# Depthwise 3x3 convolution on one core: the taps' column edges cut out of the matmuls instead of being subtracted afterwards

## The chip, the cores and the metric

The kernel runs on one core of a Trainium2 chip. The metric is device time in microseconds (us), the median of several runs. The kernel before takes 208.08 us (four runs, 207.67 to 208.5).

## What is computed

For each of 16 images and each of 128 channels (`groups = channels`, so no sum over channels) a 64x64 picture is convolved with its own 3x3 filter, zero padded by one:

```python
x_pad = np.pad(x, ((0, 0), (0, 0), (1, 1), (1, 1)))
for kh in range(3):
    for kw in range(3):
        output[b, c] += weight[c, 0, kh, kw] * x_pad[b, c, kh:kh+64, kw:kw+64]
```

A term (kh, kw) of this sum is called a tap below, written (dh, dw) as in the code. Input and output are float32.

## The kernel before

The 128 channels lie on the 128 partitions, and one image at a time is worked on. An image is loaded as one DMA that casts float32 to float16, into a row of 4096 elements (64 rows of 64) with 2 zeros in front and 2 behind (`xf`, L38 and L67 to L71; three buffers). The nine taps are shared out among three engines:

- Six taps (`PE_TAPS`, L31: all that shift by a column) are matmuls with a diagonal 128x128 matrix (`dmega`, made at the start by VectorE from an identity matrix that GpSimd writes). The image is done in two halves of 32 rows. A half is one PSUM tile `ps` of four banks (two such tiles in all, L45, which is the whole PSUM); each tap is four matmuls of 8 rows, 24 per half, 48 per image (L107). The matmul reads 512 elements in one run, shifted by one element for a column shift. At a row's end this shift reads the neighbouring row's element where the reference has a zero.
- Two taps (`ACT_TAPS`, L32: centre column, upper and lower row) are scaled copies on ScalarE into `t16` (L83; four buffers).
- The centre tap is on VectorE: `acc = xf * w + ps`, one instruction per half, which also empties PSUM (L116 for half 0, L124 for half 1).

VectorE then subtracts what the matmuls took from the neighbouring row: for each of the six taps one instruction over a single column of 63 or 64 elements, stride 64, with the negated weight `wneg` (L144). Then it adds the two ScalarE tiles (L154, twice), and GpSimd issues the store of the whole image, cast to float32 (L161; `acc` has three buffers).

Loads and stores are all issued by GpSimd, in program order of that engine: two small memsets of the pad, the load, and later the store. The order within each engine is written down at build time by a planner, which may move an instruction past others of the same engine. In the profile VectorE does image b in the order L116, second L154 of image b-1, L124, six L144, first L154. Semaphores between engines are placed by the same framework, which derives them from which instruction reads and writes which tile.

Of the kernel before, what the change touches and what calls it, by code (L numbers as in the profile page):

```python
# [1 line left out]

# [5 lines left out]


F32 = mybir.dt.float32
F16 = mybir.dt.float16


@with_exitstack
def kernel(
    ctx: ExitStack,
    tc: tile.TileContext,
    x: bass.AP,
    weight: bass.AP,  # L20
    out: bass.AP,
):
    nc = tc.nc

    B, C, H, W = x.shape
    KH = weight.shape[2]
    KW = weight.shape[3]
    assert C == 128 and KH == 3 and KW == 3 and H == 64 and W == 64
    HW = H * W

    PE_TAPS = [(1, 0), (1, 2), (0, 0), (0, 2), (2, 0), (2, 2)]  # L31
    ACT_TAPS = [(0, 1), (2, 1)]  # L32

    RG = 8
    NRG = 4
    HALF = RG * NRG

    XPAD = 2  # L38
    XLEN = XPAD + HW + 2

    consts = ctx.enter_context(tc.tile_pool(name="consts", bufs=1))
    xpool = ctx.enter_context(tc.tile_pool(name="xp", bufs=3))
    apool = ctx.enter_context(tc.tile_pool(name="acc", bufs=3))
    tpool = ctx.enter_context(tc.tile_pool(name="tt", bufs=4))
    pspool = ctx.enter_context(tc.tile_pool(name="ps", bufs=2, space=bass.MemoryType.PSUM))  # L45

    ident = consts.tile([128, 128], F32, name="ident")
    make_identity(nc, ident)

    wt = consts.tile([128, 16], F32, name="wt")  # L50
    nc.sync.dma_start(
        out=wt[:, 0:9], in_=weight.rearrange("c o kh kw -> c (o kh kw)")
    )
    wt16 = consts.tile([128, 16], F16, name="wt16")
    nc.vector.tensor_copy(out=wt16[:, 0:9], in_=wt[:, 0:9])  # L55
    wneg = consts.tile([128, 16], F32, name="wneg")
    nc.vector.tensor_scalar_mul(wneg[:, 0:9], wt16[:, 0:9], -1.0)  # L57

    dmega = consts.tile([128, 9, 128], F16, name="dmega")
    for (dh, dw) in PE_TAPS:  # L60
        k = dh * 3 + dw
        nc.vector.tensor_scalar_mul(dmega[:, k, :], ident, wt[:, k : k + 1])  # L62

    def tap_rows(dh):
        return max(0, 1 - dh), H - max(0, dh - 1)

    for b in range(B):  # L67
        xf = xpool.tile([128, XLEN], F16, name="xf")
        nc.gpsimd.memset(xf[:, 0:XPAD], 0.0)  # L69
        nc.gpsimd.memset(xf[:, XPAD + HW : XLEN], 0.0)  # L70
        nc.gpsimd.dma_start(  # L71
            out=xf[:, XPAD : XPAD + HW], in_=x[b].rearrange("c h w -> c (h w)")
        )

        acc = apool.tile([128, H, W], F16, name="acc")

        act_t = []
        for (dh, dw) in ACT_TAPS:
            k = dh * 3 + dw
            deh = dh - 1  # L80
            lo, hi = tap_rows(dh)
            t16 = tpool.tile([128, H, W], F16, name="t16")
            nc.scalar.activation(  # L83
                out=t16[:, lo:hi, :],
                in_=xf[:, XPAD + (lo + deh) * W : XPAD + (hi + deh) * W],
                func=mybir.ActivationFunctionType.Copy,
                scale=wt[:, k : k + 1],
            )
            act_t.append((t16, lo, hi))

        ps_tiles = []
        for half in range(2):
            hbase = half * HALF
            ps = pspool.tile([128, HALF, W], F32, name="ps")
            ps_tiles.append(ps)
            ntaps = len(PE_TAPS)
            for ti, (dh, dw) in enumerate(PE_TAPS):
                k = dh * 3 + dw
                deh = dh - 1
                dew = dw - 1  # L100
                lo, hi = tap_rows(dh)
                for rg in range(NRG):
                    r0 = max(hbase + rg * RG, lo)
                    r1 = min(hbase + rg * RG + RG, hi)
                    src = XPAD + (r0 + deh) * W + dew
                    n = (r1 - r0) * W
                    nc.tensor.matmul(  # L107
                        ps[:, r0 - hbase : r1 - hbase, :],
                        dmega[:, k, :],
                        xf[:, src : src + n],  # L110
                        start=(ti == 0),
                        stop=(ti == ntaps - 1),
                    )

        kC = 4
        nc.vector.scalar_tensor_tensor(  # L116
            out=acc[:, 0:HALF, :],
            in0=xf[:, XPAD : XPAD + HALF * W],
            scalar=wt[:, kC : kC + 1],
            in1=ps_tiles[0][:, :, :],  # L120
            op0=mybir.AluOpType.mult,
            op1=mybir.AluOpType.add,
        )
        nc.vector.scalar_tensor_tensor(  # L124
            out=acc[:, HALF:H, :],
            in0=xf[:, XPAD + HALF * W : XPAD + HW],
            scalar=wt[:, kC : kC + 1],
            in1=ps_tiles[1][:, :, :],
            op0=mybir.AluOpType.mult,
            op1=mybir.AluOpType.add,  # L130
        )

        for (dh, dw) in PE_TAPS:
            k = dh * 3 + dw
            deh = dh - 1
            lo, hi = tap_rows(dh)
            if dw == 0:
                col = 0
                src0 = XPAD + (lo + deh) * W - 1
            else:  # L140
                col = W - 1
                src0 = XPAD + (lo + deh) * W + W
            n = hi - lo
            nc.vector.scalar_tensor_tensor(  # L144
                out=acc[:, lo:hi, col : col + 1],
                in0=xf[:, src0 : src0 + (n - 1) * W + 1 : W],
                scalar=wneg[:, k : k + 1],
                in1=acc[:, lo:hi, col : col + 1],
                op0=mybir.AluOpType.mult,
                op1=mybir.AluOpType.add,  # L150
            )

        for (t16, lo, hi) in act_t:
            nc.vector.tensor_tensor(  # L154
                out=acc[:, lo:hi, :],
                in0=acc[:, lo:hi, :],
                in1=t16[:, lo:hi, :],
                op=mybir.AluOpType.add,
            )

        nc.gpsimd.dma_start(out=out[b], in_=acc)  # L161


# [1 line left out]
_INS = ['x', 'weight']  # L165
_OUTS = [((16, 128, 64, 64), 'float32')]


# [23 lines left out]
```

## Time and profile before

| what | us |
|---|---|
| median of four runs | 208.08 |
| the profiled execution's own time | 207.67 |
| its span, from first to last instruction | 205.7 |
| first load issued / landed | 1.34 / 9.36 |
| first matmul | 9.50 |
| last matmul ends (174.62 + 10.55) | 185.17 |
| last store issued | 197.10 |

The span holds three stretches: 9.5 us until the first image is there, some 176 us in which matmuls run, and 20.5 us behind the last matmul. In the long middle stretch an image takes 11.08 to 11.09 us, seen as the distance between one memset of the pad and the next on GpSimd. The 1.97 us between span and time lie outside of what the trace shows.

### The profile page before, as it was taken

To read this page: it belongs to the slowest core of one execution; us is meant where nothing else is said; L and a number is where in the kernel's file an instruction comes from. 1 tells how busy PE (TensorE), PEld (TensorE's weight loads), DVE (VectorE), ACT (ScalarE), POOL (GpSimd) and SP (SyncE) were. 2 spreads that over 40 slices of the span, in tenths; PEclk is the share of its full clock that TensorE was granted. 3 is DMA by queue.
4 is the path that set the end of the run, shared out by engine and by line. 5 is a ranking of instruction groups with operands and counts; after the bars stand their busy time and mean duration, and the time that the engine had idled before them with its cause. 6 is when DMAs were issued, how large, how long until landed. Compare 5 with 4: busy or idle time off the path is not lost.

```text
span 205.7 us, 1985 instructions
## 1 busy us (share of the span) xinstructions
PE 169.7 (82%) x768; PEld 74.1 (36%) x768; DVE 175.8 (85%) x168; ACT 117.9 (57%) x33; POOL 19.8 (10%) x70
## 2 busy tenths in 40 slices
PE   0199999999998989898999989898989898990000
PEld 0044444444443434343434434343434343440000
DVE  2004899999999999999999999999999999999920
ACT  2199658484848576775848484848677674800000
POOL 5000011111111101011111111110101110101010
PEclk9999999999999999999999999999999999999555
DMA  4995069999999999999999999899999993452745
GB/s 71 215 215 112 0 99 300 285 237 352 209 384 182 408 182 379 198 351 233 293 284 279 315 239 343 177 424 175 386 198 347 233 333 156 175 233 102 306 204 204
DMA packets 4761, 50.46 MB, mean 245 GB/s; under 512 B 656, under 2 KB 656, under 8 KB 656
## 3 DMA queue, kind: packets, MB, share of 16 engines
q0 software_dynamic: 4608, 50.33, 84.3%
q8 instruction: 6, 0.10, 0.2%
q1 hardware_dynamic: 144, 0.00, 0.0%
q14 instruction: 3, 0.02, 0.0%
HBM read 33.56 MB, written 33.55 MB: 326 GB/s over the span
## 4 chain that ended last, share of the span: by engine, by line
DVE 43%; issue 42%; PE 6%; DMA 4%; POOL 1%; POOLq 0%; DVEq 0%
DVE acc L154 15%; DVE acc L124 14%; DVE acc L144 12%; PE ps L107 6%; DMA xf<-in_x_dram 4%; DVE acc L116 1%; POOL out_dram L161 1%; POOLq L187 0%; DVEq L154 0%; DVEq L144 0%; POOL ident masks.py:197 0%; POOL xf L69 0%; POOL xf L70 0%; POOLq L161 0%; POOLq masks.py:199 0%
## 5 line engine op out<-in xcount | busy, mean ns | idle before, releaser
L107 PE MATMUL ps<-xf,dmega 128*128 128x512 f16 (+1 forms) x768 | 169.7, 380 | 15.5 <-DMA xf<-in_x_dram 9.5
L83 ACT ACTIVATE t<-xf,wt 128x4032 f16<-128x4032 f16 x32 | 116.7, 3654 | 60.1 <-DVE acc L154 54.4
L107 PEld LDWEIGHTS <-dmega 128*128 128x128 f16 x768 | 74.1, 98 | 110.6 <-DVE acc L116 11.6
L154 DVE TENSOR_TENSOR acc<-acc,t 128x4032 f16<-128x4032 f16 x32 | 72.2, 2256 | 1.8
L116 DVE SCALAR_TENSOR_TENSOR acc<-xf,wt,ps 128x2048 f16<-128x2048 f16 x16 | 37.5, 2342 | 12.4 <-PE ps L107 12.4
L124 DVE SCALAR_TENSOR_TENSOR acc<-xf,wt,ps 128x2048 f16<-128x2048 f16 x16 | 37.5, 2343 | 2.8 <-PE ps L107 2.8
L144 DVE SCALAR_TENSOR_TENSOR acc<-xf,wneg,acc 128x63 f16<-128x63 f16 (+1 forms) x96 | 30.9, 532 | 1.6
L161 POOL DMA_DIRECT2D out_dram<-acc x16 | 8.6, 536 | 105.2 <-DVE acc L154 105.2
L71 POOL DMA_DIRECT2D xf<-in_x_dram x16 | 8.7, 542 | 4.9 <-issue 4.9
L69 POOL MEMSET xf<- 128x2 f16 x16 | 1.7, 105 | 67.2 <-DVE acc L144 63.5
L83 ACT ACT_TABLE_LOAD x1 | 1.3, 1283 | 2.4 <-DMA wt<-in_weight_dram 2.4
L55 DVE CAST wt<-wt 128x9 f16<-128x9 f32 x1 | 0.2, 185 | 2.3 <-DMA wt<-in_weight_dram 2.3
L70 POOL MEMSET xf<- 128x2 f16 x16 | 1.6, 99 | 0.0
L62 DVE TENSOR_SCALAR dmega<-ident,wt 128x128 f16<-128x128 f32 x6 | 1.3, 297 | 0.0
masks.py:199 POOL TENSOR_SCALAR_AFFINE_SELECT ident<-ident 128x128 f32<-128x128 f32 x1 | 0.3, 304 | 0.1
masks.py:197 POOL MEMSET ident<- 128x128 f32 x1 | 0.2, 204 | 0.3 <-POOLq L176 0.3
L57 DVE TENSOR_SCALAR wneg<-wt 128x9 f32<-128x9 f16 x1 | 0.2, 174 | 0.0
L176 POOL MEMSET const-float32-0.0<- 128x1 f32 x1 | 0.1, 98 | 0.2 <-issue 0.2
L176 POOL MEMSET const-float32-1.0<- 128x1 f32 x1 | 0.1, 98 | 0.0
L176 POOL MEMSET const-bfloat16-1.0<- 128x1 bf16 x1 | 0.1, 98 | 0.0
L176 POOL MEMSET const-uint8-127<- 128x1 uint8 x1 | 0.1, 98 | 0.0
## 6 DMA issues: line engine op xcount, KB each, us to landing
out_dram<-acc POOLq DMA_DIRECT2D x16, 2048.0 KB, 6.6
xf<-in_x_dram POOLq DMA_DIRECT2D x16, 1024.0 KB, 8.0
wt<-in_weight_dram SPq DMA_DIRECT2D x1, 4.5 KB, 1.6
```

Of the source, the lines that this page charges most:

```text
L62: nc.vector.tensor_scalar_mul(dmega[:, k, :], ident, wt[:, k : k + 1])
L69: nc.gpsimd.memset(xf[:, 0:XPAD], 0.0)
L70: nc.gpsimd.memset(xf[:, XPAD + HW : XLEN], 0.0)
L71: nc.gpsimd.dma_start(out=xf[:, XPAD : XPAD + HW], in_=x[b].rearrange("c h w -> c (h w)"))
L83: nc.scalar.activation(out=t16[:, lo:hi, :], in_=xf[:, XPAD + (lo + deh) * W : XPAD + (hi + deh) * W], func=mybir.ActivationFunctionType.Copy,
L107: nc.tensor.matmul(ps[:, r0 - hbase : r1 - hbase, :], dmega[:, k, :], xf[:, src : src + n], start=(ti == 0), stop=(ti == ntaps - 1),)
L116: nc.vector.scalar_tensor_tensor(out=acc[:, 0:HALF, :], in0=xf[:, XPAD : XPAD + HALF * W], scalar=wt[:, kC : kC + 1], in1=ps_tiles[0][:, : ...
L124: nc.vector.scalar_tensor_tensor(out=acc[:, HALF:H, :], in0=xf[:, XPAD + HALF * W : XPAD + HW], scalar=wt[:, kC : kC + 1], in1=ps_tiles[1] ...
L144: nc.vector.scalar_tensor_tensor(out=acc[:, lo:hi, col : col + 1], in0=xf[:, src0 : src0 + (n - 1) * W + 1 : W], scalar=wneg[:, k : k + 1] ...
L154: nc.vector.tensor_tensor(out=acc[:, lo:hi, :], in0=acc[:, lo:hi, :], in1=t16[:, lo:hi, :], op=mybir.AluOpType.add,)
L161: nc.gpsimd.dma_start(out=out[b], in_=acc)
L176: nc = _bacc.Bacc("TRN2", target_bir_lowering=False, num_devices=1)
```

## The change

Three things are changed.

First, the column shift. A matmul of a tap with dw = 0 now writes only columns 1 to 63 of its 8 rows, one with dw = 2 only columns 0 to 62, so input and output are 8 runs of 63 elements and nothing has to be subtracted: the six instructions of L144 go. For the rows' edges the pad in front of and behind the image becomes 66 elements of zeros, so that every matmul has all of its 8 rows. The tap (0, 1), which needs no cut, goes to TensorE, as its first tap; (0, 0) goes to ScalarE, which writes columns 1 to 63 into one of three tiles of their own whose column 0 is set to zero once at the start (`tedge`). The adds and copies go over 4096 elements where they went over 4032.

Second, the first image's load is cut in two DMAs: 34 rows, then 30.

Third, the last image is finished and stored by halves: per half the centre tap, two adds over half of the tile, and a store of half the image.

```diff
-    PE_TAPS = [(1, 0), (1, 2), (0, 0), (0, 2), (2, 0), (2, 2)]
-    ACT_TAPS = [(0, 1), (2, 1)]
+    PE_TAPS = [(0, 1), (1, 0), (1, 2), (0, 2), (2, 0), (2, 2)]
+    ACT_TAPS = [(0, 0), (2, 1)]
...
-    XPAD = 2
-    XLEN = XPAD + HW + 2
+    XPAD = W + 2
+    XLEN = XPAD + HW + W + 2
...
+    tedge = []
+    for i in range(3):
+        te = consts.tile([128, H, W], F16, name=f"tedge{i}")
+        nc.vector.memset(te[:, :, 0:1], 0.0)
+        tedge.append(te)
...
+        xsrc = x[b].rearrange("c h w -> c (h w)")
+        if first:
+            nsplit = (HALF + 2) * W
+            nc.gpsimd.dma_start(out=xf[:, XPAD : XPAD + nsplit], in_=xsrc[:, 0:nsplit])
+            nc.gpsimd.dma_start(out=xf[:, XPAD + nsplit : XPAD + HW], in_=xsrc[:, nsplit:HW])
+        else:
+            nc.gpsimd.dma_start(out=xf[:, XPAD : XPAD + HW], in_=xsrc)
...
-            lo, hi = tap_rows(dh)
-            t16 = tpool.tile([128, H, W], F16, name="t16")
+            lo = 1 if dw == 0 else 0
+            t16 = tedge[b % 3] if dw == 0 else tpool.tile([128, H, W], F16, name="t16")
+            xrow = xf[:, XPAD + deh * W : XPAD + deh * W + HW]
             nc.scalar.activation(
-                out=t16[:, lo:hi, :],
-                in_=xf[:, XPAD + (lo + deh) * W : XPAD + (hi + deh) * W],
+                out=t16[:, :, lo:W],
+                in_=xrow.rearrange("c (h w) -> c h w", w=W)[:, :, 0 : W - lo],
...
+                lo, hi_c = (1, W) if dw == 0 else (0, W - 1) if dw == 2 else (0, W)
                 for rg in range(NRG):
...
+                    base = XPAD + (hbase + rg * RG + dh - 1) * W
+                    rows = xf[:, base : base + RG * W].rearrange("c (r w) -> c r w", w=W)
                     nc.tensor.matmul(
-                        ps[:, r0 - hbase : r1 - hbase, :],
+                        ps[:, rg * RG : rg * RG + RG, lo:hi_c],
                         dmega[:, k, :],
-                        xf[:, src : src + n],
+                        rows[:, :, lo + dw - 1 : hi_c + dw - 1],
...
-        for (dh, dw) in PE_TAPS:
...
-            nc.vector.scalar_tensor_tensor(
-                out=acc[:, lo:hi, col : col + 1],
-                in0=xf[:, src0 : src0 + (n - 1) * W + 1 : W],
-                scalar=wneg[:, k : k + 1],
-                in1=acc[:, lo:hi, col : col + 1],
...
+        for hi, (h0, h1) in enumerate([(0, HALF), (HALF, H)]):
             nc.vector.scalar_tensor_tensor(
+                out=acc[:, h0:h1, :],
+                in0=xf[:, XPAD + h0 * W : XPAD + h1 * W],
+                scalar=wt[:, kC : kC + 1],
+                in1=ps_tiles[hi][:, :, :],
...
+            if last:
+                for t16 in act_t:
+                    nc.vector.tensor_tensor(
+                        out=acc[:, h0:h1, :],
+                        in0=acc[:, h0:h1, :],
+                        in1=t16[:, h0:h1, :],
+                        op=mybir.AluOpType.add,
+                    )
+                nc.gpsimd.dma_start(out=out[b][:, h0:h1, :], in_=acc[:, h0:h1, :])
+        if not last:
+            for t16 in act_t:
+                nc.vector.tensor_tensor(
+                    out=acc, in0=acc, in1=t16, op=mybir.AluOpType.add
+                )
+            nc.gpsimd.dma_start(out=out[b], in_=acc)
```

## Rows read from the trace of the kernel before

**Rows 1.** The page, part 1: busy time, share of the span, instructions of each engine.

```profile
PE 169.7 (82%) x768; PEld 74.1 (36%) x768; DVE 175.8 (85%) x168; ACT 117.9 (57%) x33; POOL 19.8 (10%) x70
```

**Rows 2.** VectorE's timeline, one period: start us, us, instruction, count, idle before.

```profile
50.27 2.34 DVE L116 SCALAR_TENSOR_TENSOR acc<-xf,wt,ps 128x2048 f16<-128x2048 f16 x1
52.53 2.25 DVE L154 TENSOR_TENSOR acc<-acc,t 128x4032 f16<-128x4032 f16 x1
54.69 2.34 DVE L124 SCALAR_TENSOR_TENSOR acc<-xf,wt,ps 128x2048 f16<-128x2048 f16 x1
57.14 1.94 DVE L144 SCALAR_TENSOR_TENSOR acc<-xf,wneg,acc 128x64 f16<-128x64 f16 x6
59.18 2.26 DVE L154 TENSOR_TENSOR acc<-acc,t 128x4032 f16<-128x4032 f16 x1
61.36 2.34 DVE L116 SCALAR_TENSOR_TENSOR acc<-xf,wt,ps 128x2048 f16<-128x2048 f16 x1
```

**Rows 3.** TensorE's timeline, one image in the middle and the last one.

```profile
97.03 10.55 PE L107 MATMUL ps<-xf,dmega 128*128 128x512 f16 x48 [0.55 <-DVE acc L116]
...
174.62 10.55 PE L107 MATMUL ps<-xf,dmega 128*128 128x512 f16 x48 [0.55 <-DVE acc L116]
```

**Rows 4.** Stretches of L107 on TensorE: A:B, length, busy, granted clock, DMA share, GB/s.

```profile
9.50:13.00 3.50, 3.50 (x10) 1.00 0.99 208
...
21.50:50.00 28.50, 28.50 (x133) 1.00 0.78 222
```

**Rows 5.** GpSimd's timeline: the identity's mask, one period, the last store.

```profile
2.10 0.30 POOL masks.py:199 TENSOR_SCALAR_AFFINE_SELECT ident<-ident 128x128 f32<-128x128 f32 x1
...
59.31 0.10 POOL L69 MEMSET xf<- 128x2 f16 x1 [3.71 <-DVE acc L144]
...
59.79 0.53 POOL L71 DMA_DIRECT2D xf<-in_x_dram  x1 [0.35 <-issue]
66.16 0.54 POOL L161 DMA_DIRECT2D out_dram<-acc  x1 [5.85 <-DVE acc L154]
70.39 0.10 POOL L69 MEMSET xf<- 128x2 f16 x1 [3.69 <-DVE acc L144]
...
197.10 0.53 POOL L161 DMA_DIRECT2D out_dram<-acc  x1 [8.47 <-DVE acc L154]
```

**Rows 6.** Stretches, all engines: loads alone, a store alone, the middle; DMA share, GB/s last.

```profile
5.00:18.00 13.00, 8.50 (x33) 3.60 (x34) 1.68 (x1) 8.62 (x3) 0.00 (x0) 1.00 1.04 217
...
198.00:203.10 5.10, 0.00 (x0) 0.00 (x0) 0.00 (x0) 0.00 (x0) 0.00 (x0) 0.50 1.01 411
59.31:170.20 110.89, 105.51 (x482) 45.94 (x480) 108.81 (x101) 73.12 (x20) 11.92 (x40) 1.00 0.99 285
```

**Rows 7.** The chain that ended last, its start: start us, us, what.

```profile
1.34 8.02 DMA xf<-in_x_dram
...
9.50 11.98 PE ps L107 x48
...
21.50 2.36 DVE acc L124
```

**Rows 8.** VectorE's timeline, its last adds (both of them in one row).

```profile
192.19 4.62 DVE L154 TENSOR_TENSOR acc<-acc,t 128x4032 f16<-128x4032 f16 x2
```

**Rows 9.** The page, part 6: DMA issues, KB each, median us to landing.

```profile
out_dram<-acc POOLq DMA_DIRECT2D x16, 2048.0 KB, 6.6
xf<-in_x_dram POOLq DMA_DIRECT2D x16, 1024.0 KB, 8.0
```

**Rows 10.** Groups by line, shapes apart: busy us, mean ns, idle before.

```profile
L144 DVE SCALAR_TENSOR_TENSOR acc<-xf,wneg,acc 128x63 f16<-128x63 f16 x64 | 22.1, 532 | 0.0
```

**Rows 11.** ScalarE's timeline, the two copies of one image.

```profile
83.65 3.65 ACT L83 ACTIVATE t<-xf,wt 128x4032 f16<-128x4032 f16 x1 [3.01 <-DVE acc L154]
88.08 3.66 ACT L83 ACTIVATE t<-xf,wt 128x4032 f16<-128x4032 f16 x1 [0.77 <-DVE acc L154]
```

More of the change, by code (lines that the diff above doesn't have):

```diff
@@ L62 @@
         nc.vector.tensor_scalar_mul(dmega[:, k, :], ident, wt[:, k : k + 1])
-    def tap_rows(dh):
-        return max(0, 1 - dh), H - max(0, dh - 1)
+    tedge = []
[3 more added lines that the diff above has]
+        tedge.append(te)
     for b in range(B):
+        first = b == 0
+        last = b == B - 1
         xf = xpool.tile([128, XLEN], F16, name="xf")
@@ L70 @@
         nc.gpsimd.memset(xf[:, XPAD + HW : XLEN], 0.0)
-        nc.gpsimd.dma_start(
-            out=xf[:, XPAD : XPAD + HW], in_=x[b].rearrange("c h w -> c (h w)")
-        )
+        xsrc = x[b].rearrange("c h w -> c (h w)")
[5 more added lines that the diff above has]
+            nc.gpsimd.dma_start(out=xf[:, XPAD : XPAD + HW], in_=xsrc)
         acc = apool.tile([128, H, W], F16, name="acc")
@@ L88 @@
             )
-            act_t.append((t16, lo, hi))
+            act_t.append(t16)
         ps_tiles = []
@@ L98 @@
                 k = dh * 3 + dw
-                deh = dh - 1
-                dew = dw - 1
-                lo, hi = tap_rows(dh)
+                lo, hi_c = (1, W) if dw == 0 else (0, W - 1) if dw == 2 else (0, W)
                 for rg in range(NRG):
[L103 to L106, printed above, removed]
+                    base = XPAD + (hbase + rg * RG + dh - 1) * W
+                    rows = xf[:, base : base + RG * W].rearrange("c (r w) -> c r w", w=W)
                     nc.tensor.matmul(
-                        ps[:, r0 - hbase : r1 - hbase, :],
+                        ps[:, rg * RG : rg * RG + RG, lo:hi_c],
                         dmega[:, k, :],
-                        xf[:, src : src + n],
+                        rows[:, :, lo + dw - 1 : hi_c + dw - 1],
                         start=(ti == 0),
@@ L115 @@
         kC = 4
-        nc.vector.scalar_tensor_tensor(
[L117 to L131, printed above, removed]
-        for (dh, dw) in PE_TAPS:
[L134 to L143, printed above, removed]
+        for hi, (h0, h1) in enumerate([(0, HALF), (HALF, H)]):
             nc.vector.scalar_tensor_tensor(
-                out=acc[:, lo:hi, col : col + 1],
-                in0=xf[:, src0 : src0 + (n - 1) * W + 1 : W],
-                scalar=wneg[:, k : k + 1],
-                in1=acc[:, lo:hi, col : col + 1],
+                out=acc[:, h0:h1, :],
+                in0=xf[:, XPAD + h0 * W : XPAD + h1 * W],
+                scalar=wt[:, kC : kC + 1],
+                in1=ps_tiles[hi][:, :, :],
                 op0=mybir.AluOpType.mult,
@@ L151 @@
             )
[L153 to L161, printed above, removed]
+            if last:
[13 more added lines that the diff above has]
+            nc.gpsimd.dma_start(out=out[b], in_=acc)
 _INS = ['x', 'weight']
```

## The prediction

> **What bounds the kernel now.** I read the busy times first, then the timelines of VectorE and TensorE over one period, then the two ends of the span. No engine is full by its share: TensorE 82%, VectorE 85% [rows 1]. The timelines say which of the two sets the pace. VectorE's instructions follow each other without a gap that the view would show, from L116 at 50.27 to the next L116 at 61.36: 11.09 us, made of two evacuations, two adds and six column fixes [rows 2]. TensorE runs 48 matmuls in 10.55 us and then sits 0.55 us, each time until VectorE's L116 has emptied a PSUM tile [rows 3]. So VectorE is the bound by half a microsecond per image, with TensorE right behind it. GpSimd confirms the period: pad memset to pad memset, 59.31 to 70.39, is 11.08 us [rows 5]. The DMA engines stand at a share of 0.99 over the middle [rows 6], which has to be watched. At the front TensorE waits 9.50 us for the first load [rows 7]; at the end the last add and a whole store lie behind the last matmul [rows 5, 8].
>
> **What the column fixes are worth.** The six fixes take 0.53 us each by their own durations [rows 10], but they overlap: from the first L144 at 57.14 to the L154 behind it at 59.18 are 2.04 us [rows 2]. Without them VectorE needs 11.09 - 2.04 = 9.05 us, plus two adds over 4096 in place of 4032 elements (2.26 x 64/4032 = 0.04 us each): 9.13 us. An add that follows another add on the same tile costs 4.62/2 = 2.31 us [rows 8], an evacuation followed by an instruction that needs it 2.45 us (54.69 to 57.14) [rows 2]; if the planner puts all four in program order the sum is 2 x 2.45 + 2 x 2.35 = 9.6 us. Either is under TensorE's 10.4 us below, so only the first 0.7 us of the 2 us show: **TensorE becomes the bound**.
>
> Does TensorE then wait for VectorE nevertheless? With two PSUM tiles it may start half 0 of the next image when L116 of this one is done. In program order VectorE does, after half 1's end, the evacuation and two adds, 2.45 + 4.70 = 7.15 us, while the next half 0 is ready after 5.2 us; its evacuation starts 1.95 us late and ends 4.3 us after it became ready, within the 5.2 us that TensorE needs for the other half. That leaves 0.9 us. In the alternating order of now there is no lateness. I cost the handover at nothing.
>
> **TensorE's period.** 28.50 us held 132 starts or so with no wait [rows 4], and (10.55 - 0.38)/47 in a later image [rows 3] says the same, 216 ns per matmul, nearly all of 512 columns. After the change 40 matmuls have 8 x 63 = 504 columns and 8 have 512. By the columns the 40 would take 216 x 504/512 = 213 ns; if the eight runs cost nothing and the column count is not felt either, 216. I take 216, the row: 48 x 0.216 = 10.37 us per image. No row shows a matmul that writes PSUM in runs. Its bounds are 210 ns (504 columns at the 2.4 GHz which the granted clock of 1.00 means), which gives 10.1 us, and the slowest stretch there is: 10 matmuls in the first 3.50 us, 350 ns each [rows 4], 15.7 us per image. I stay with the nearest row, since the shifted input of now already starts at odd elements and runs at 216 ns.
>
> The Trainium skill speaks against that: "Advanced Engine Details and Errata", section PSUM Cachelines, says that PSUM is organised in lines of two float32 values, that any non-contiguous access slows matmuls significantly, and that every two consecutive elements should be contiguous. No row tests it, since each output of now is one run. Taken by its first half it is the slower rival below; by its second half 62 of 63 elements still pair up and nothing changes.
>
> **The front.** Loads alone move 217 GB/s as written [rows 6]; a load is 1.05 MB, so 4.83 us of its 8.02 us are data [rows 7]. The first part holds 34 of 64 rows, so it lands 30/64 x 4.83 = 2.26 us earlier, and the first matmul starts at 9.50 - 2.3 = 7.2 us. Bounds: 5.7 (if all 8.02 us scale) and 9.8 (if the framework makes half 0 wait for both parts; the extra issue of 0.5 us then counts). The second part lands before 10, half 0 lasts until 14, so it is hidden. The extra DMA issue, 0.53 us, and the larger pad memsets (0.10 us now [rows 5]; at most the 0.30 us that the mask over 128 elements takes) are ahead of the next loads, and perhaps ahead of the identity's mask at 2.10 [rows 5], from which VectorE makes the diagonals: 0.5 to 0.9 us later is still ahead of 7.2. In later images the memsets are hidden by the loads' lead of two images. The three memsets of a column for `tedge` are some 64 strided elements each, like a fix, at most 0.53 us [rows 10], while VectorE waits for TensorE: nothing. The first image takes 11.98 us [rows 7], 1.6 us above the period, as its opening stretch is slow; I keep that.
>
> **ScalarE** makes two copies of 3.65 us per image and waits 3.8 us [rows 11]. The cut copy has as many elements as now, the other 4096: 7.4 us, and the cover of 3 us takes 40% more. Its tiles come free later than they are needed: three `tedge`, and four `t16` of which an image now takes one.
>
> **The end.** Call E the last matmul's end. VectorE gets half 1 of image 14 at E - 10.37 and then has: evacuation 2.45, two adds 4.70, evacuation 2.45, two half adds 2.35, evacuation 2.45, two half adds 2.35 = 16.75 us, so E + 6.4 (the two earlier stores of this image and of image 14 are issued on the way, the first half's behind its adds on GpSimd, where nothing but the second half's waits behind it). From the last add to the store's issue now 196.81 to 197.10, 0.29 us; a store lands 6.6 us later [rows 9], of which 5.1 us are data [rows 6], so half a store needs 6.6 - 2.55 = 4.05 us; from landing (197.10 + 6.6) to the end of the span 205.7 are 2.0 us. The end is E + 12.7, where it is 205.7 - 185.17 = 20.5 us now.
>
> **The sum.** E = 7.2 + 11.98 + 15 x 10.37 = 174.7 us; span 187.4; plus the 1.97 us between the profiled span and its own time of 207.67: **189.4 us**. That time is the lowest of the four runs, 0.4 below the median. Front, middle and end give 2.3, 15 x 0.7 = 10.7 (less some of the head's ramp) and 7.8 us, some of which overlap with waits of today: 18.3 in all.
>
> **Do the DMAs allow it?** A share of 0.99 over 11.09 us is 10.97 us per load and store [rows 6]. But a load alone is 4.83 us of data and a store 5.1, together 9.9; the rest are slow first packets after a gap, as load and store now take turns with little overlap (issues 6.4 and 4.2 us apart [rows 5]). If 11.09 per pair were a hard limit: the fourth load's data starts at about 7.2 + 11.98 + 2.36 + 1.4 = 22.9 us, then 13 pairs x 11.09 and three stores x 5.1 end at 182.4, the span at about 185. That is still not later than 187.4, because the DMAs idle less at both ends. So they are a co-limit at worst, and the load's lead hides the rest. They take over when a pair needs more than 11.3 us (rival 4).
>
> **Rivals.**
> 1. *The period stays.* Not VectorE's count but something else in the loop, DMA pairs that get slower when they overlap or the handover of PSUM tiles, holds 11.09 us. For it: the 0.99 share, and the lead of only 0.9 us. Against: the 9.9 us of data per pair, and that TensorE's only wait is for L116. Time: 7.2 + 11.98 + 166.4 + 12.7 + 1.97 = 200.2 us; with pairs stretched by half of that excess, 195.
> 2. *Whole tiles are waited for.* If the first matmul waits for both parts of the first load: 9.8 in place of 7.2, 192.0 us. That the change would not do what it says in this one place is likelier than elsewhere, since no row shows a wait on part of a tile.
> 3. *Cut matmuls are slower*, the one that ends slower than before. Place: the 40 matmuls with eight runs of 63 float32 in PSUM. A run is odd, so every second one starts at an odd place in the stream; if such a row takes twice as long, a matmul takes 324 ns, the image 40 x 0.324 + 8 x 0.216 = 14.7 us, and the time is 7.2 + 16.3 + 15 x 14.7 + 11.1 (VectorE no longer late at the end) + 1.97 = 257 us. It decides from 207.67 - 1.97 - 12.7 - 7.2 - 1.6 = 184.2 = 16 periods, 11.5 us: 245 ns per cut matmul, 29 ns or 3.6 ns per row more than now. Against it: the stream reads from odd elements at full rate today.
> 4. *The DMAs become the bound.* Load and store overlap more when the period shrinks, and may slow each other. By the chain above the time is 42.8 + 13 times the pair: equal to the forecast at 11.3 us, 199 at 12.0. For it: the 10.97 us of share against 9.9 of data; against: that a store alone writes 411 GB/s, and loads alone read twice the 217 that they write [rows 6]. The Trainium skill, "DMA: Bandwidth & Descriptors", section Where 436 GB/s comes from, has a rule for it: about 358 GB/s per core between HBM and SBUF; with 4.19 MB per pair that is 11.7 us, an estimate of 195 for the time. The rows of loads and of stores alone lie above that limit.
>
> **Chances.** The forecast, 184 to 193 us with rival 2 in it (0.12 of it): 0.65. Rival 1, 193 to 201: 0.11. Rival 4, in the same stretch: 0.05. Rival 3: 0.17, of which 0.12 slower than before, 0.02 within 0.3% (about what a measurement of this kernel tells from no change) and 0.03 still faster. Some other wait, still faster: 0.02. So faster 0.86, same 0.02, slower 0.12. The range 183 to 201 leaves out little more than rival 3; the forecast's own is 184 to 193.
>
> **What would show it.** Right: TensorE's timeline without a wait for L116 and 48 matmuls every 10.2 to 10.5 us; VectorE busy about 9.2 us of it and waiting for `ps`; first matmul near 7.2; the last store's issue some 6.7 us behind the last matmul. Wrong: a mean pitch of matmuls above 220 ns (rival 3, and the cut taps alone would show it), TensorE idle before L107 with VectorE or a DMA as releaser (rival 1), a first matmul after 9.5 (rival 2).

## The result and the profile after

The changed kernel takes 191.63 us (median of 11 runs, 191.11 to 192.68) where the one before takes 208.28 (16 runs, 207.33 to 208.91): ratio 0.921, interval 0.9189 to 0.9232, 16.6 us less. The forecast was 189.4 in a range of 183 to 201; the measured median is 2.2 us above it.

First the page of the changed kernel, the busy times that answer to [rows 1].

```profile
span 190.4 us, 1873 instructions
...
PE 170.1 (89%) x768; PEld 75.5 (40%) x768; DVE 149.2 (78%) x77; ACT 117.0 (61%) x33; POOL 22.7 (12%) x72
```

VectorE has lost 26.6 us of work and 91 instructions; TensorE is as busy as it was, in a shorter span. Its whole timeline is one line, where [rows 3] had a line and a wait for each image:

```profile
7.38 170.10 PE L114 MATMUL ps<-xf,dmega 128*128 128x512 f16 x768 [7.38 <-DMA xf<-in_x_dram]
```

Once it has begun TensorE waits for nothing until 177.48. VectorE now is the one that waits, as its timeline over one period shows (beside [rows 2]):

```profile
52.16 2.35 DVE L124 SCALAR_TENSOR_TENSOR acc<-xf,wt,ps 128x2048 f16<-128x2048 f16 x1 [1.05 <-PE ps L114]
54.61 2.29 DVE L143 TENSOR_TENSOR acc<-acc,tedge 128x4096 f16<-128x4096 f16 x1
57.01 2.29 DVE L143 TENSOR_TENSOR acc<-acc,t 128x4096 f16<-128x4096 f16 x1
59.22 2.34 DVE L124 SCALAR_TENSOR_TENSOR acc<-xf,wt,ps 128x2048 f16<-128x2048 f16 x1
62.61 2.35 DVE L124 SCALAR_TENSOR_TENSOR acc<-xf,wt,ps 128x2048 f16<-128x2048 f16 x1 [1.05 <-PE ps L114]
```

The planner put VectorE's four instructions per image (two evacuations of PSUM, two adds) in program order; from L124 to L124 of the same half are 10.45 us, of which 1.05 is a wait for TensorE. The two ends, on GpSimd, beside [rows 5]:

```profile
1.50 0.67 POOL L80 DMA_DIRECT2D xf<-in_x_dram  x1
2.17 0.54 POOL L81 DMA_DIRECT2D xf<-in_x_dram  x1
...
174.51 0.53 POOL L146 DMA_DIRECT2D out_dram<-acc  x1 [9.91 <-DVE acc L143]
179.42 0.53 POOL L140 DMA_DIRECT2D out_dram<-acc  x1 [4.38 <-DVE acc L134]
184.20 0.53 POOL L140 DMA_DIRECT2D out_dram<-acc  x1 [4.24 <-DVE acc L134]
```

And the opening of VectorE, from which the first image can be read: its two evacuations start when TensorE ends a half.

```profile
15.60 2.35 DVE L124 SCALAR_TENSOR_TENSOR acc<-xf,wt,ps 128x2048 f16<-128x2048 f16 x1 [11.46 <-PE ps L114]
20.82 2.35 DVE L124 SCALAR_TENSOR_TENSOR acc<-xf,wt,ps 128x2048 f16<-128x2048 f16 x1 [2.87 <-PE ps L114]
```

The first image thus takes 20.82 - 7.38 = 13.44 us, not the 11.98 of before [rows 7]: in this execution TensorE started 2.1 us earlier than in the one profiled before and finished the first image only 0.7 us earlier.

| term | forecast | measured |
|---|---|---|
| first matmul | 7.2 | 7.38 |
| first image | 11.98 | 13.44 |
| 15 periods | 15 x 10.37 = 155.5 | 15 x 10.447 = 156.7 |
| last matmul's end E | 174.7 | 177.48 |
| from E to the span's end | 12.7 | 12.9 |
| span | 187.4 | 190.4 |

The profiled execution's own time is 192.37 us, 1.97 above its span as before. The 3.0 us by which the span is over the forecast's are the first image (1.5), the period (1.2), and 0.2 at each end.

### The profile page after: what moved, and what is told of

Read it like the earlier page. It is cut to its first block, busy times and chain, and to the rows that moved or that the text cites. A ratio compares the mean times of both kernels' runs of the same rounds, so it can differ in the third digit from the quotient of the medians.

```text
span 190.4 us, 1873 instructions
## 1 busy us (share of the span) xinstructions
PE 170.1 (89%) x768; PEld 75.5 (40%) x768; DVE 149.2 (78%) x77; ACT 117.0 (61%) x33; POOL 22.7 (12%) x72
## 4 chain that ended last, share of the span: by engine, by line
PE 73%; issue 15%; DVE 4%; DMA 3%; POOL 1%; POOLq 0%; DVEq 0%
PE ps L114 73%; DMA xf<-in_x_dram 3%; DVE acc L143 2%; DVE acc L124 1%; POOL out_dram L146 1%; POOLq L172 0%; POOL out_dram L140 0%; POOL ident masks.py:199 0%; POOL xf L75 0%; POOL xf L76 0%; POOL ident masks.py:197 0%; DVEq L143 0%; POOLq L140 0%; POOLq L146 0%; POOLq L161 0%
## 5 line engine op out<-in xcount | busy, mean ns | idle before, releaser
L114 PE MATMUL ps<-xf,dmega 128*128 128x504 f16 (+1 forms) x768 | 170.1, 384 | 7.4 <-DMA xf<-in_x_dram 7.4
L114 PEld LDWEIGHTS <-dmega 128*128 128x128 f16 x768 | 75.5, 98 | 101.5 <-issue 11.1
L124 DVE SCALAR_TENSOR_TENSOR acc<-xf,wt,ps 128x2048 f16<-128x2048 f16 x32 | 75.0, 2345 | 29.0 <-PE ps L114 29.0
L94 ACT ACTIVATE tedge<-xf,wt 128x4032 f16<-128x4032 f16 x16 | 58.4, 3653 | 38.0 <-DMA xf<-in_x_dram 37.9
L94 ACT ACTIVATE t<-xf,wt 128x4096 f16<-128x4096 f16 x16 | 59.1, 3693 | 0.0
L143 DVE TENSOR_TENSOR acc<-acc,tedge 128x4096 f16<-128x4096 f16 x15 | 34.4, 2292 | 1.6
L143 DVE TENSOR_TENSOR acc<-acc,t 128x4096 f16<-128x4096 f16 x15 | 34.4, 2292 | 1.6
L146 POOL DMA_DIRECT2D out_dram<-acc x15 | 8.0, 537 | 71.5 <-DVE acc L143 71.5
L75 POOL MEMSET xf<- 128x66 f16 x16 | 2.6, 161 | 78.2 <-issue 54.3
L76 POOL MEMSET xf<- 128x66 f16 x16 | 2.6, 163 | 0.0
L134 DVE TENSOR_TENSOR acc<-acc,t 128x2048 f16<-128x2048 f16 x2 | 2.4, 1224 | 0.1
L134 DVE TENSOR_TENSOR acc<-acc,tedge 128x2048 f16<-128x2048 f16 x2 | 2.4, 1224 | 0.1
L140 POOL DMA_DIRECT2D out_dram<-acc x2 | 1.1, 531 | 8.6 <-DVE acc L134 8.6
```

The source lines that it names most:

```text
L94: nc.scalar.activation(out=t16[:, :, lo:W], in_=xrow.rearrange("c (h w) -> c h w", w=W)[:, :, 0 : W - lo], func=mybir.ActivationFunctionTy ...
L114: nc.tensor.matmul(ps[:, rg * RG : rg * RG + RG, lo:hi_c], dmega[:, k, :], rows[:, :, lo + dw - 1 : hi_c + dw - 1], start=(ti == 0), stop= ...
L124: nc.vector.scalar_tensor_tensor(out=acc[:, h0:h1, :], in0=xf[:, XPAD + h0 * W : XPAD + h1 * W], scalar=wt[:, kC : kC + 1], in1=ps_tiles[h ...
L134: nc.vector.tensor_tensor(out=acc[:, h0:h1, :], in0=acc[:, h0:h1, :], in1=t16[:, h0:h1, :], op=mybir.AluOpType.add,)
L140: nc.gpsimd.dma_start(out=out[b][:, h0:h1, :], in_=acc[:, h0:h1, :])
L143: nc.vector.tensor_tensor(out=acc, in0=acc, in1=t16, op=mybir.AluOpType.add)
```

## The experiments

The theory: three independent parts, the column fixes in the middle (TensorE takes over as the bound), an earlier start, a shorter end; and the two missed terms are a slow opening of TensorE and a mis-read price of a matmul. The rivals are those of the forecast: DMAs or PSUM handover as the bound, dear cut matmuls, ends that were hidden anyway. All ratios are to the kernel before on the same chip. e5 to e8 are one execution each and are read by their traces, not by their times.

**e1, the column edges alone.**

```diff
-        first = b == 0
-        last = b == B - 1
+        first = False
+        last = False
```

> The changed kernel with the first load and the last store whole again: only the column edges are changed. If the three parts of the change work each in its own stretch: first matmul at about 9.6 us, first image 12.0, period 10.45, E = 9.6 + 12.0 + 15 x 10.45 = 178.4; behind E VectorE needs 6.3 us, then 0.3, a whole store 6.6 and 2.0: span 193.7, time about 195.6, 4 us above the changed kernel. If the ends were hidden anyway (the early start is lost again in the slow opening, the store's half beside other stores): within 1 us of the changed kernel's 191.6.

197.43 us, ratio 0.9453 (0.9407 to 0.9499). The first matmul starts at 9.82, the period is again 10.45 (from VectorE's evacuation at 22.91 to the one at 179.61 are 15 of them), TensorE's line is

```profile
9.82 169.75 PE L114 MATMUL ps<-xf,dmega 128*128 128x512 f16 x768 [9.82 <-DMA xf<-in_x_dram]
```

and VectorE's evacuations of the second half, in the first and in the last image, are

```profile
22.91 2.35 DVE L124 SCALAR_TENSOR_TENSOR acc<-xf,wt,ps 128x2048 f16<-128x2048 f16 x1 [2.88 <-PE ps L114]
...
179.61 2.35 DVE L124 SCALAR_TENSOR_TENSOR acc<-xf,wt,ps 128x2048 f16<-128x2048 f16 x1 [1.05 <-PE ps L114]
```

so E is 179.57, and the span ends 16.0 us behind it. The ends are worth 5.8 us beside the changed edges by the medians and 5.2 by the two profiled spans, so they were not hidden. The miss of 1.8 us is instructive: the first image took 13.1 us here (22.91 - 9.82), though it starts only 0.3 us later than that of before, and the end is longer than a count of VectorE's work gave (15.2), because the last evacuation cannot start before E: 2.45 + 4.6 + 0.3 + 6.6 + 2.0 = 16.

**e2, the kernel before without the fixes.**

```diff
-        for (dh, dw) in PE_TAPS:
...
-            nc.vector.scalar_tensor_tensor(
-                out=acc[:, lo:hi, col : col + 1],
...
```

> The kernel before without the six column instructions of L144; its output is wrong in columns 0 and 63. If VectorE's fixes set the period and TensorE is next: 48 x 216 ns = 10.4 us, E = 9.5 + 12.0 + 15 x 10.4 = 177.5, end E + 15.1, time about 194.6. If the DMAs or the handover of PSUM hold the period at 11.09 (rival 1): only the 2 us of the last image go, about 206. Beside e1 it gives the price of the cut matmuls themselves: 1.0 us for 1.4 ns per matmul (217.6 in the changed kernel against 216.2), and much more if a run in PSUM costs what rival 3 says.

196.02 us, ratio 0.9395 (0.9355 to 0.9435), a period of 10.375 us (15 of them between the two evacuations shown). TensorE again runs in one piece; below its line are VectorE's evacuations of the second half, in the first and in the last image:

```profile
9.54 167.59 PE L107 MATMUL ps<-xf,dmega 128*128 128x512 f16 x768 [9.54 <-DMA xf<-in_x_dram]
...
21.55 2.35 DVE L124 SCALAR_TENSOR_TENSOR acc<-xf,wt,ps 128x2048 f16<-128x2048 f16 x1 [2.84 <-PE ps L107]
...
177.16 2.35 DVE L124 SCALAR_TENSOR_TENSOR acc<-xf,wt,ps 128x2048 f16<-128x2048 f16 x1 [1.04 <-PE ps L107]
```

So the fixes alone held the period, and rival 1 falls. The expectation of 194.6 is missed by 1.4 us: the end is 16.0 us for 15.1, as in e1, and the median lies 0.9 above the profiled execution. e1, with its cut matmuls, is 1.4 us above it; in the profiled executions it is 2.5, of which 15 x 0.07 = 1.1 are the period, 1.1 the first image (13.1 against 12.0) and 0.3 the start.

**e3, the two ends alone,** with the column fixes kept.

```diff
+        if b == 0:
+            nsplit = (HALF + 2) * W
+            nc.gpsimd.dma_start(out=xf[:, XPAD : XPAD + nsplit], in_=xsrc[:, 0:nsplit])
+            nc.gpsimd.dma_start(out=xf[:, XPAD + nsplit : XPAD + HW], in_=xsrc[:, nsplit:HW])
...
+        if last:
+            for half in range(2):
+                h0 = half * HALF
+                center(half)
+                fixes(h0, h0 + HALF)
+                adds(h0, h0 + HALF)
+                nc.gpsimd.dma_start(out=out[b][:, h0 : h0 + HALF, :], in_=acc[:, h0 : h0 + HALF, :])
```

> The kernel before with the first load in two parts and the last image finished and stored by halves; the column fixes stay, in the last image twice six over half a column. If the opening of TensorE ends at a time of its own, near 12.7 us, whenever it starts: half 0 done some 0.7 us earlier, at the end 2.5 us less store but 2 us more of column fixes: 206 to 207. If the early start counts in full and the fixes by halves are short: 208.3 - 2.1 - 2.5 = 203.7. If the ends alone made the 18 us of the forecast's 2.3 + 7.8: 198.

204.98 us, ratio 0.9831 (0.9795 to 0.9867): 3.8 us less, between the two theories. VectorE's opening:

```profile
15.60 2.35 DVE L124 SCALAR_TENSOR_TENSOR acc<-xf,wt,ps 128x2048 f16<-128x2048 f16 x1 [11.55 <-PE ps L111]
20.78 2.35 DVE L124 SCALAR_TENSOR_TENSOR acc<-xf,wt,ps 128x2048 f16<-128x2048 f16 x1 [2.84 <-PE ps L111]
```

As in the changed kernel 2.1 us of earlier start (7.42) become 0.7 us (20.78 against 21.50 in [rows 7]), here with uncut matmuls, so the cut has nothing to do with it (e4 says what has). At the other end the last store's issue is where it was (197.13 against 197.10), 2.3 us of store are saved, and the period keeps 11.08. In the two profiled executions the spans differ by 2.3 us, in the medians the times by 3.8. The 1.5 between them lies in which execution was profiled: that of before, 207.67, is 1.15 below the median of 208.82, that of e3, 205.23, 0.25 above its own. (The third figure expected, 198, is 208.3 less the 10.1 of the forecast's two ends; the 18 in it is a slip.) The sum of e1 and e3, 11.4 + 3.8 = 15.2, is near the 16.6 of all together.

**e4, TensorE busy before the first load lands.**

```diff
+    warm = consts.tile([128, 512], F16, name="warm")
+    nc.vector.memset(warm, 0.0)
+    psw = pspool.tile([128, HALF, W], F32, name="ps")
+    for i in range(13):
+        nc.tensor.matmul(psw[:, 0:RG, :], warm[:, 0:128], warm, start=True, stop=True)
```

> The changed kernel with 13 more matmuls of zeros, 512 columns each, into a PSUM tile that nothing reads, from about 1.7 us on while the first load is under way. If TensorE's slow opening (13.4 us for the first image in place of 10.45, matmuls of about 0.4 us until 12.7 us) comes from its having been idle before: the first image takes 10.5 to 10.8, E comes 2.7 us earlier, time 188.8. If it comes from something else at that time, as the three loads running beside it: 191.6 as in the changed kernel, or up to 1 us more if the added matmuls hold up the first real one.

189.67 us, ratio 0.9099 (0.9068 to 0.9129). TensorE's timeline, and below it VectorE's evacuation that follows the first image:

```profile
2.04 4.52 PE L74 MATMUL ps<-warm 128*128 128x512 f16 x13 [2.04 <-DVE warm L71]
7.39 167.31 PE L120 MATMUL ps<-xf,dmega 128*128 128x512 f16 x768 [0.83 <-DMA xf<-in_x_dram]
...
18.03 2.35 DVE L130 SCALAR_TENSOR_TENSOR acc<-xf,wt,ps 128x2048 f16<-128x2048 f16 x1 [2.88 <-PE ps L120]
```

The start is the same, 7.39, but the 768 matmuls take 167.31 us in place of 170.10, and the first image, up to this evacuation, 18.03 - 7.39 = 10.64. The 13 empty ones took 348 ns each in their turn. The slow opening comes from TensorE's idleness before it, not from the loads beside it, which run on as before. My notion in e3 that it ends at a time of its own, near 12.7 us, falls: in e1, which starts at 9.82, TensorE still ran 6 matmuls (with those cut by the window's edges) from 11.82 to 13.82 and 8 from there to 15.82 (start and end, length, busy time and matmuls, granted clock, DMA share, GB/s):

```profile
9.82:11.82 2.00, 2.00 (x5) 1.00 1.04 217
11.82:13.82 2.00, 2.00 (x6) 1.00 1.10 229
13.82:15.82 2.00, 2.00 (x8) 1.00 1.00 209
15.82:17.82 2.00, 2.00 (x11) 1.00 0.98 205
```

That is half the pace of later (11 with edges), though the column of the granted clock reads 1.00. The column does not show the clock there: each trace's entries of it begin with a rise to 1.00, at 12.46 us before, 13.12 in the changed kernel, 14.84 in e1 and 5.19 in e4, just where the pace changes, and the column counts the time ahead of the first entry as 1.00. In the middle of e8 (below) there are entries. After 16.8 us without a matmul TensorE starts at 114.80, and the same two paces come with a clock of 0.50 (1.2 GHz) and 1.00 (2.4 GHz):

```profile
116.00:118.00 2.00, 2.00 (x6) 0.50 1.00 209
118.00:120.00 2.00, 2.00 (x6) 0.50 0.94 197
120.00:122.00 2.00, 2.00 (x11) 1.00 1.15 242
```

So the slow opening has the pace of the lower level, and what it has in common with this stretch is that TensorE stood idle before. That it belongs to the first matmuls of a program falls, too.

First image less one period is 1.6 us before and in e2, 3.0 in the changed kernel and in e3, 2.6 in e1, 2.5 in e5. The traces' starts of matmuls show why: with 504 or 512 columns, from one to the next are 427 ns in the slow stretch and 215 to 220 behind it, and there are 7 slow ones before and in e2, 12 in e1, 14 in the changed kernel and in e3. That an earlier start makes the stretch longer is not shown: e1 starts latest and has 12, e8 starts at 7.59 as e5 does and has 8 where e5 has 11, and the 13 matmuls of zeros, begun between 2.03 and 2.14 us in e4, e9 and e10 (below), took 4.52, 5.16 and 5.73 us:

```profile
2.03 5.16 PE L74 MATMUL ps<-warm 128*128 128x512 f16 x13 [2.03 <-DVE warm L71]
2.14 5.73 PE L79 MATMUL ps<-warm 128*128 128x512 f16 x13 [2.14 <-DVE warm L76]
```

So its length changes from execution to execution at the same start; by what, these runs do not tell. Beside e1, with the same matmuls, the changed kernel starts 2.4 us earlier and ends its first image 2.1 us earlier (20.82 against 22.91).

**e5, the matmuls uncut**: 512 columns in one run.

```diff
-                        ps[:, rg * RG : rg * RG + RG, lo:hi_c],
+                        ps[:, rg * RG : rg * RG + RG, :],
                         dmega[:, k, :],
-                        rows[:, :, lo + dw - 1 : hi_c + dw - 1],
+                        xf[:, base + dw - 1 : base + dw - 1 + RG * W],
```

> The changed kernel with all matmuls of 512 columns in one run, in and out, as before; its output is wrong at the columns' edges. It prices the eight runs. If runs cost nothing and a matmul has a fixed part of some 5 ns beside its columns: 512/2.4 + 5 = 218 ns, period 10.45 or a little more. If the runs cost the 1.4 ns by which the changed kernel's pitch of 217.6 stands above the 216.2 of before: 216, period 10.38, about 1 us less. If rival 3 had any large part in it: below 210, which the column count excludes at 2.4 GHz.

192.52 us in one execution, a period of 10.475 us, the mean of 13 between the first evacuation shown and the one at 167.21:

```profile
31.04 2.35 DVE L124 SCALAR_TENSOR_TENSOR acc<-xf,wt,ps 128x2048 f16<-128x2048 f16 x1 [1.08 <-PE ps L114]
...
41.52 2.35 DVE L124 SCALAR_TENSOR_TENSOR acc<-xf,wt,ps 128x2048 f16<-128x2048 f16 x1 [1.08 <-PE ps L114]
```

A matmul of 512 columns in one run is 10.475/48 = 218.2 ns, dearer than a cut one: (10.447 - 8 x 0.2182)/40 = 217.5. For 448 columns in one run the kernel before has rows, since four of its 48 matmuls per image lack a row; its groups by shape in the stretch of [rows 4], mean ns in the middle:

```profile
L107 PE MATMUL ps<-xf,dmega 128*128 128x512 f16 x123 | 28.6, 380 | 0.0
L107 PE MATMUL ps<-xf,dmega 128*128 128x448 f16 x10 | 3.5, 352 | 0.0
```

These durations overlap, but they are 28 ns apart. With e2's period, 10.375 for 44 of the one and 4 of the other, that makes 218.5 and 190.5 ns; the starts of the matmuls in e2's trace say 218.4 and 190.9. So columns count, some 27 ns for 64 of them, and eight columns less would be about 214.8: the eight runs cost some 2.7 ns, 0.3 each.

**e6, runs of 56 columns**.

```diff
-                lo, hi_c = (1, W) if dw == 0 else (0, W - 1) if dw == 2 else (0, W)
+                lo, hi_c = (8, W) if dw == 0 else (0, W - 8) if dw == 2 else (0, W)
```

> The changed kernel with runs of 56 columns in place of 63 (448 columns, even starts; the output is wrong in the columns left out). If the pitch goes by the columns: 448/2.4 + 7 = 194 ns for 40 matmuls, 9.5 us per image while nothing else holds it, read in the first images; then VectorE (9.6 in program order) or the DMAs (9.9 to 11) become the bound and the time falls to 180 to 186. If a matmul costs the same whatever its columns: 10.45, 191.6. If odd starts cost something, the pitch falls by more than the 23 ns of the columns.

179.37 us in one execution. VectorE's evacuations, the two of the first image and those of the second half in the second and the fourth:

```profile
14.85 2.35 DVE L124 SCALAR_TENSOR_TENSOR acc<-xf,wt,ps 128x2048 f16<-128x2048 f16 x1 [10.76 <-PE ps L114]
19.64 2.35 DVE L124 SCALAR_TENSOR_TENSOR acc<-xf,wt,ps 128x2048 f16<-128x2048 f16 x1 [2.44 <-PE ps L114]
...
29.21 2.35 DVE L124 SCALAR_TENSOR_TENSOR acc<-xf,wt,ps 128x2048 f16<-128x2048 f16 x1 [0.18 <-PE ps L114]
...
48.46 2.35 DVE L124 SCALAR_TENSOR_TENSOR acc<-xf,wt,ps 128x2048 f16<-128x2048 f16 x1 [0.18 <-PE ps L114]
```

In the first image, where nothing waits, half 1 takes 4.79 us (14.85 to 19.64): (4.79 - 4 x 0.2182)/20 = 195.9 ns for 448 columns in eight even runs, 5 ns above the 190.9 of the same columns in one run (e5), or 4 where matmuls at the same place in their tap are compared. So odd starts cost nothing that even ones do not. From there on two periods take 19.25 us (29.21 to 48.46), 9.62 each. VectorE's program order was forecast at 9.6 and is 9.4 with 0.2 to 0.3 of wait, and TensorE needs 8 x 218.2 + 40 x 195.9 ns = 9.58 us: which of the two holds the period the run does not tell. The DMAs follow (their share and GB/s last):

```profile
30.00:155.00 125.00, 125.00 (x625) 58.92 (x624) 119.34 (x53) 95.33 (x27) 16.20 (x49) 1.00 1.04 324
```

324 GB/s as written, against 285 in [rows 6], at much the same share. A pair of load and store goes through in 9.6 us; rival 4 falls. So the share near 1 in [rows 6] was not a limit: at much the same share more bytes went through.

**e7, every second word of PSUM** (five of six taps have 256 columns, half 0 in one run, half 1 with step 2).

```diff
+                         ps[:, rg * RG : rg * RG + RG // 2, :] if half == 0 else
+                         ps[:, rg * RG : rg * RG + RG, 0:W:2]),
```

> The changed kernel in which five of six taps have 256 columns: in half 0 as one run in PSUM, in half 1 as every second word of PSUM; the input is one run in both (the output is wrong). Two half images in one trace, alike but for the step in PSUM. If TensorE writes every second word at full rate: both halves 4 x 217 + 20 x 112 = 3.1 us. If two words make one access, so that a step of two costs double, as rival 3 has it: half 1 takes 4 x 217 + 20 x 218 = 5.2 us.

188.32 us in one execution, held by waits that this order brought. The question is answered by TensorE's timeline, where single halves stand alone:

```profile
44.27 3.25 PE L114 MATMUL ps<-xf,dmega 128*128 128x512 f16 x24 [0.85 <-DVE acc L127]
48.72 5.35 PE L114 MATMUL ps<-xf,dmega 128*128 128x512 f16 x24 [1.21 <-DVE acc L127]
55.22 3.24 PE L114 MATMUL ps<-xf,dmega 128*128 128x512 f16 x24 [1.15 <-DVE acc L127]
```

Half 0 takes 3.24 us, half 1 5.35: 2.1/20 = 105 ns more per matmul of 256 columns. In the first image half 1 takes 5.18 us from evacuation to evacuation (13.12 to 18.30), (5.18 - 4 x 0.2182)/20 = 215 ns for such a matmul, so 110 in one run: twice the price. So a doubling as in rival 3 exists; it is met by single words, not by long runs.

**e8, less work on the engines, the same transfers** (four taps on TensorE, one on ScalarE).

```diff
-    PE_TAPS = [(0, 1), (1, 0), (1, 2), (0, 2), (2, 0), (2, 2)]
-    ACT_TAPS = [(0, 0), (2, 1)]
+    PE_TAPS = [(0, 1), (1, 0), (1, 2), (0, 2)]
+    ACT_TAPS = [(0, 0)]
```

> The changed kernel with four taps on TensorE and one on ScalarE in place of six and two (the output lacks three terms), all loads and stores as they are: TensorE needs 7.0 us per image, VectorE 7.2, ScalarE 3.7, so the DMAs should be the bound. If a pair of load and store is 4.83 + 5.1 us of data and the rest is waiting: 10.0 us per image, time about 166. If a pair costs the 10.97 us that the share of 0.99 gave in the kernel before: 182. At 11.3 or more (rival 4) the changed kernel would already be held by them: 187.

187.83 us in one execution, which would speak for rival 4 if the timeline were not read. The planner ordered GpSimd anew, with loads behind stores:

```profile
103.12 0.53 POOL L146 DMA_DIRECT2D out_dram<-acc  x1 [6.43 <-DVE acc L143]
...
103.82 0.54 POOL L83 DMA_DIRECT2D xf<-in_x_dram  x1
...
104.52 0.56 POOL L83 DMA_DIRECT2D xf<-in_x_dram  x1
...
105.22 0.56 POOL L83 DMA_DIRECT2D xf<-in_x_dram  x1
127.06 0.15 POOL L75 MEMSET xf<- 128x66 f16 x1 [21.28 <-DVE acc L124]
```

Three loads go out together as soon as a store's wait is over, then none for 22 us, and VectorE stands for 18.2 us:

```profile
121.02 2.35 DVE L124 SCALAR_TENSOR_TENSOR acc<-xf,wt,ps 128x2048 f16<-128x2048 f16 x1 [18.20 <-PE ps L114]
```

The run prices an order, not the DMAs; e6 settles what it was meant for.

**e9 and e10, towards a faster kernel.** e9 is e4 in which three matmuls per image leave out the row that only multiplies zeros; e10 also takes one matmul of 48 off TensorE, as a small copy on ScalarE and a small add on VectorE.

```diff
+                    if (dh, dw) == (2, 0) and hbase + rg * RG + RG == H:
+                        continue
+                    r0, r1 = rg * RG, rg * RG + RG
+                    if ti > 0 and dh == 0 and hbase + r0 == 0:
+                        r0 += 1
+                    if dh == 2 and hbase + r1 == H:
+                        r1 -= 1
...
+        nc.scalar.activation(
+            out=sm[:, :, 1:W],
...
+            nc.vector.tensor_tensor(
+                out=acc[:, H - RG : H, :], in0=acc[:, H - RG : H, :], in1=sm, op=mybir.AluOpType.add
+            )
```

> e4 (the changed kernel with 13 early matmuls of zeros) in which three matmuls per image drop the row that only multiplies zeros: tap (0, 2) the image's first, taps (2, 0) and (2, 2) its last, so 7 runs of 63 = 441 columns. If the kernel before had its 216 ns per matmul from its four matmuls of 448 columns beside 44 at 218 (e5), each shortened matmul gains some 26 ns, the period falls from 10.45 to 10.37 and the time by 1.2 us to 188.4. If the column count is not felt in a stream of longer matmuls: 189.6 as e4.

> e9 with one matmul of 48 taken from TensorE: the last eight rows of tap (2, 0) are a small scaled copy on ScalarE (512 elements, about 0.6 us) and a small add on VectorE (some 0.38 us). If TensorE alone bounds the loop and VectorE's program order of 9.6 us leaves room: period 10.37 - 0.22 = 10.15, time 188.4 - 3.3 = 185.2. If VectorE's order or its handover of PSUM comes up first (its 9.6 + 0.4 = 10.0 us, and each late evacuation holds the next half): period 10.3 or more, time 187.5 to 189. If the DMAs hold it (e6 ran 9.6 us per image, so not expected): no gain.

e9: 188.43 us, ratio 0.9043 (0.9018 to 0.9069), a period of 10.36 (evacuations at 59.63 and 69.99): the columns are felt. e10: 185.98 us, ratio 0.8928 (0.8901 to 0.8954), clear of both kernels, 5.7 us under the changed one. Its period:

```profile
58.95 2.35 DVE L150 SCALAR_TENSOR_TENSOR acc<-xf,wt,ps 128x2048 f16<-128x2048 f16 x1 [0.44 <-PE ps L140]
...
68.26 0.42 DVE L176 TENSOR_TENSOR acc<-acc,tsm 128x512 f16<-128x512 f16 x1
69.13 2.35 DVE L150 SCALAR_TENSOR_TENSOR acc<-xf,wt,ps 128x2048 f16<-128x2048 f16 x1 [0.44 <-PE ps L140]
```

10.18 us, with 0.44 us of VectorE's wait left: TensorE still is the bound. One more matmul moved would take 0.2 us off it and put 0.4 on VectorE, by this row's 0.42; that closes the gap, and the estimate is that little is left to gain that way.

## Why the prediction was right, and where it was off

*VectorE's fixes set the period, and TensorE is next.* Right: without them alone (e2) the period goes from 11.09 to 10.375 us, with the change to 10.447. The 2 us of fixes give 0.65 to 0.7 us per image, as TensorE is the next to bound the loop, and VectorE waits 1.05 us.

*The period, 48 x 216 ns.* The mis-sized term, by 0.08 us or 1.2 in all. The forecast took 216 as what a matmul costs "if the eight runs cost nothing and the column count is not felt either". Both halves of that are off: the 216 of [rows 3, 4] was a mean of 44 matmuls at 218.5 and 4 of 448 columns at 190.5 (e5, e2). The change brought the latter to full rows. In a cut matmul the eight columns less save 3.4 ns and the eight runs cost 2.7 (e5); that the two nearly cancel is luck, since the forecast had a row for neither. The groups by shape shown at e5 are of the trace of before: by them the row could have been split beforehand.

*The cut matmuls, rival 3.* Not what happened: a cut matmul takes 217.5 ns. The Trainium skill, "Advanced Engine Details and Errata", section PSUM Cachelines, says both that any non-contiguous access is slow and that every two consecutive elements should be contiguous. The runs bear out the second: 3.24 against 5.35 us for single words (e7). The first is too wide: rows of 63 words cost 1%, odd starts included.

*The front.* The first matmul at 7.38 is the 7.2 of the forecast, so half 0 waits for the first part of the load only, and rival 2 falls. But the step "The first image takes 11.98 us [rows 7] ... I keep that" failed: it took 13.44. The row came from an execution with 7 slow matmuls at the opening; the profiled execution of the changed kernel has 14, e3 as many with the old matmuls, and e4 removes them from the first image by work ahead of it. The forecast took as fixed what changes from execution to execution. That the earlier start costs anything is not shown (e1 lost 2.6 us at 9.82), and most of this miss is the draw of the two profiled executions: by the medians the gain is 16.6 us where the forecast has 18.3, and the period's 1.2 and 0.2 at each end make up nearly all of the difference.

*The end.* 12.9 us against 12.7, worked from the same rows: VectorE's last adds at E + 6.4, the half store 4.1 us to landing.

*The DMAs.* They kept up, 9.6 us per pair in e6, with longer landings (median 10.4 us for a load and 10.7 for a store, where [rows 9] has 8.0 and 6.6). The forecast called them a co-limit at worst; they are not one down to 9.6 us. In e6 they move 4.19 MB per 9.62 us, 436 GB/s read and written. The Trainium skill's 358 GB/s ("DMA: Bandwidth & Descriptors", Where 436 GB/s comes from) does not hold for a core that runs alone, as the single streams of [rows 6] had suggested.

## What to carry to other kernels

Take the next engine's price per instruction by shape, not as a mean of a group, before it becomes the bound; here a twelfth of shorter matmuls hid 2 ns in each of the others. Do not carry the first image's time of one profiled execution into a forecast as fixed: TensorE opens slowly after idling, for a stretch that changes from execution to execution. Give it empty work while the first load is under way. A DMA share of 0.99 is not shown to be a limit until a run with less compute shows that the period stops there, and such a run must keep the order of the queues.

## What the runs showed of the hardware that was not expected

TensorE's first matmuls after it stood idle start 427 ns apart in place of 215 to 220, for 3 to 6 us, at the opening of a program and in the middle of e8, where the granted clock of that stretch reads 0.50. The loss of the first image lies between 1.6 and 3.0 us. With 13 matmuls of zeros ahead it is 0.2 in e4; in e10, whose slow stretch was the longest, the first real matmul still falls into it, and the loss is 0.4. The times also lie closer together: 189.63 to 189.87 in four runs of e4, 191.11 to 192.68 in the eleven of the changed kernel. That the opening makes this spread is only argued, and e10, with the same zeros, spreads over 0.6 us in four runs.

A matmul that writes every second word of PSUM takes twice as long (110 to 215 ns at 256 columns), one that writes eight runs of 63 words 2.7 ns more than the same columns in one run, and eight of 56 words 4 to 5 ns more.
